# A fourth Strassen unit in the last gate pair, x1's third and fourth quarters ahead of the splits, and the third output group in other banks

## The chip, the cores and the metric

The kernel runs on one core of one Trainium2 chip. The metric is device time in microseconds (us) per execution, the median of the runs; the kernel before takes 807.91 us (three runs, 807.77 to 809.03). Besides the runs there is one profiled execution, whose trace all rows come from. The engines are named as in the profile: PE multiplies matrices (PEld loads its weights), DVE, ACT and POOL work on vectors, SP issues DMA transfers.

## The reference

One layer of a hybrid decoder for 256 tokens of width 2048, all float32. Cut to what matters here:

```python
h = rmsnorm(x, norm_mix_g)
c_g, b_g, xa, za, q, fl, iv, og, ga, gb = split(h @ w_in)
ya = b_g * causal_dwconv3(c_g * xa, conv_w) * silu(za)
log_f = logaddexp(log(lb), log1p(-lb) + log_sigmoid(fl))
kk = (1 - lb) * sigmoid(-fl)
yb = rmsnorm_per_head(hgrn2_chunked(silu(q), kk, iv, log_f)) * silu(og)
m = sigmoid(ga) * (ya @ w_a_out) + sigmoid(gb) * (yb @ w_b_out)
x1 = x + m @ w_o
x2 = x1 + sigmoid(rmsnorm(x1, ple_norm_g) @ w_ple_gate) * (p @ w_ple_proj)
out = rmsnorm(x2, final_norm_g)
```

The change touches the last part of it, from `m @ w_o` to the output, and at one place the `fl` branch.

## The kernel before, in words

**Precision and matmuls.** Each float32 operand is held as two numbers of a shorter type, hi and lo = x - hi, and a product is three matmuls: hi by hi, hi by lo, lo by hi. Activations are the stationary side (128 x 128; names `xh`, `xl` for x1, `mh`, `ml` for m), weights the moving side, 512 columns at a time (`whi`, `wlo`). The 256 tokens are two tiles t = 0, 1, and the 2048 columns of a projection are groups of 512, numbered j.

**Weights.** They stream from memory as `raw` tiles of 1 MB, two chunks of K = 256 each, in three buffers; a new transfer waits until DVE has read the buffer three back. `split` turns a chunk into `whi` on ACT (line 166) and `wlo` on DVE (line 167). Lines 119 to 131 issue the transfers on SP.

**Stages** at the end, in the order of PE's work: OO (output groups 0 and 1 together), O2, O3 (groups 2 and 3 alone), PG0 (gate group 0), GP (gate groups 1 and 2 together), PG3. In the plain groups a chunk is 12 matmuls (line 1258). A stage that takes two groups together follows a written-out program (here `LATE`, line 47) of units (line 1280): `(u, c)` is two chunks for group u, `(2, c)` is one chunk for both, each 24 matmuls; `("S", c)` is one chunk for both groups in Strassen's way: seven products instead of eight, 21 matmuls. For it DVE combines weights in place (`combine_weights`, lines 181, 184, 185), the unit's chunk is split into four parts (three of 1024 columns, one, `t2`, of 512), and the activations enter as *forms* (`So0`, `So1`), which `forms` makes from x1's quarters 0 and 1, one set for each S unit that uses that quarter.

**Sums.** Products of a pair are gathered in banks of two kinds of PSUM tiles, `g` and `s`; `sums` (line 849) adds them up on DVE (the operations appear under `add`, line 845), step by step, as they are finished. For GP `ep_gates_late` then hands each group to `gated` (line 1008): sigmoid on ACT (line 1014), product with `pw` and addition to x (lines 1017, 1018, DVE), squares (line 1019, ACT), and multiplication by the final gain on POOL (line 1026). PG3's first matmuls take over a bank that the first add of GP's sums has read.

**x1's quarters.** When output group j is ready, `ep_o` (line 941) adds it to x (line 845), spreads it (line 947, ACT), takes squares (line 954), and `turned` transposes: four transfers out on SP (line 346, `turn<-t`), one back (line 350, `t<-turn`), and a transposition of 32 x 32 blocks on DVE (line 354). For quarters 2 and 3 `put` then makes `xh` (line 310, ACT) and `xl` (line 311, DVE), four each.

**What sets the order.** Each engine runs its instructions in the order in which they are issued. An epilogue is a generator; the main loop calls `advance` about once per chunk, and every `yield` is a turn's delay; the argument `lag` of `turned` is the number of turns between the way back and the transposition. Splits run ahead of their matmuls by several chunks (`ahead`). For positions in the list of ranges `tied`, `split` is issued after both instructions in `state["splits"]`, the last split before it. Elsewhere a scheduler may place them.

The functions that the change touches, with the line numbers of the profile:

Of the kernel before, what the change touches and what calls it, by code (L numbers as in the profile page):

```python
# [11 lines left out]
AF = mybir.ActivationFunctionType  # L12
# [4 lines left out]
T = 256  # L17
NT = T // P
# [25 lines left out]
INNER = (0, 4), ("S", 0), (0, 6), ("S", 1), (2, 3), ("S", 2), (1, 4), (1, 6)  # L44
FRONT = (0, 2), (0, 4), (0, 6), ("S", 0), (1, 2), ("S", 1), (1, 4), (1, 6)
OUT = (0, 4), ("S", 0), (1, 4), ("S", 1), (2, 3), ("S", 2), (0, 6), (1, 6)
LATE = (0, 4), ("S", 0), (0, 6), ("S", 1), (2, 3), ("S", 2), (1, 4), (1, 6)


PRM_GMIX, PRM_GPLE, PRM_GHG, PRM_LB, PRM_CONV = 0, 16, 32, 40, 48  # L50
# [5 lines left out]
def hybrid_kernel(ctx, tc, xT, x, pT, prm, gfin, masks, w_in, w_a, w_b, w_o, w_pg, w_pp, out):  # L56
    nc = tc.nc
# [23 lines left out]
    state = {"tmp": "tmp1"}  # L81
# [11 lines left out]
    def bank(tag):  # L93
        return ps.tile([P, CW], F32, tag=tag, bufs=4, name=nm(tag))
# [145 lines left out]
    gates, late = of_kind("GG"), of_kind("PG")[0]  # L240
# [6 lines left out]
    tied = []  # L247
# [4 lines left out]
    closing = last_unit("OO", OUT)  # L252
    last = range(gates[-1] + 1, closing + 1)
    outer = range(closing + 6, of_kind("O")[-1] + 1)
    tied.append(range(last[0] - 4, outer[-1] + 1))
    inner = [of_kind(kind) for kind in ("QV", "VG")]
    inner = range(inner[0][0] - 3, inner[0][-1] + 1), range(inner[1][0] - 6, inner[1][-1] + 1)

# [27 lines left out]
    def gain(base, k):  # L286
        return prm_t[:, base + k : base + k + 1]
# [15 lines left out]
    def put(op, k, src, scale=None):  # L303

        hi, lo = op[0][:, k, :], op[1][:, k, :]
        if scale is None:
            nc.scalar.activation(out=hi, in_=src, func=AF.Copy)
            nc.vector.tensor_tensor(out=lo, in0=src, in1=hi.bitcast(F32), op=ALU.subtract)
        else:
            nc.scalar.activation(out=hi, in_=src, func=AF.Identity, scale=scale)  # L310
            nc.vector.scalar_tensor_tensor(  # L311
                out=lo, in0=src, scalar=scale, in1=hi.bitcast(F32), op0=ALU.mult, op1=ALU.subtract
            )


    def rsqrt_of(ss, n, width, tag):
# [20 lines left out]
    def turned(src, lag, dst=None):  # L337

        d = dram.tile([P, 4, T], F32, tag="turn", bufs=3, name=nm("turn"))
        to = d.rearrange("(b i) a x -> a i b x", b=4)
        for a in range(4):
            state["sent"] = nc.sync.dma_start(
                out=to[a], in_=src[32 * a : 32 * a + 32, :].rearrange("i (b x) -> i b x", b=4)
            ).ins
        yield
        nc.sync.dma_start(out=src, in_=d.rearrange("p a x -> p (a x)"))  # L350
        for _ in range(lag):
            yield
        dst = t4() if dst is None else dst
        nc.vector.transpose(  # L354
            out=dst.rearrange("p (k a e) -> p a k e", a=4, e=32), in_=src.rearrange("p (a k e) -> p a k e", a=4, e=32)
        )
        return dst
# [37 lines left out]
    def ep_f(j, psum):  # L395
# [3 lines left out]
        sg = t4()  # L399
# [4 lines left out]
        one, low = (state[n][:, j * 4 : j * 4 + 4] for n in ("oml", "lbm"))  # L404
        for h in range(4):
            s = slice(h * T, (h + 1) * T)
            nc.vector.tensor_scalar(
                out=sg[:, s], in0=sg[:, s], scalar1=one[:, h : h + 1], scalar2=low[:, h : h + 1],
                op0=ALU.mult, op1=ALU.add,
            )  # L410
# [5 lines left out]
            )  # L416
        yield
        yield


        lf, last = t4(), sc(8, "lfl", 2)
        lv, fv = segments(lf), segments(sg)
# [518 lines left out]
    def ep_o(j, psum):  # L941
        xs = state["x"]
        x1 = t4()
        for t in range(NT):
            d = xs[:, t, j * CW : (j + 1) * CW]
            add(d, d, psum[t])
            nc.scalar.activation(out=spread(x1, t), in_=blocks(d), func=AF.Copy)
        turn = turned(x1, 6 if j == 1 else 2)
        next(turn)
        yield  # L950
        junk = t4()
# [18 lines left out]
            yield from forms("x1T", form_tiles(pools["tmp3"], f"So{j}", len(chunks)), r, chunks)  # L970
            return
        for c in range(4):
            put(state["x1T"], j * 4 + c, x1[:, c * T : (c + 1) * T], gain(PRM_GPLE, j * 4 + c))
        if j == 3:
            tot = sc(2, "tot2", 1)
            nc.vector.tensor_reduce(
# [341 lines left out]
    psum = None  # L1318
    for pos, (gi, c) in enumerate(steps[:last_group]):
# [80 lines left out]
                load_projection(1 + c[0] // 2)  # L1400
            continue
        if c == 0:
            psum = [bank("s" if kind == "PP" and j > 1 else "g") for _ in range(NT)]
        hi, lo = parts.pop(pos)
        for i in range(2):
            k = 2 * c + i
# [134 lines left out]
```

## Time and profile before

| | |
|---|---|
| median of three runs | 807.91 us (807.77 to 809.03) |
| the profiled execution | 809.07 us |
| its span, from first to last instruction | 807.3 us |
| mean clock granted to PE | 0.996 |
| busy: PE | 798.0 us, 4169 matmuls |
| busy: DVE | 685.1 us |
| busy: ACT | 492.1 us |
| busy: POOL | 95.4 us |
| HBM over the span | 236 GB/s |

A row of the timeline is: start in us, length in us of the group, engine, line, operation, output <- inputs, shapes, and how many instructions of one kind stand together (xN); in brackets the idle time of the engine ahead of it and what ended that. Matmuls overlap, so their lengths add to more than the time; the distance between starts tells the pace. Rows of transfers give how many, KB each, and us from issue to landing. Rows of stretches give the length, then the busy time and the count of PE, PEld, DVE, ACT and POOL, the granted clock, the share of the DMA engines, and GB/s.

### The profile page before, as it was taken

Reading aid. Unit: us, or ns where it says so; the run is one execution under the profiler, and the core shown is the slowest. Engines: PE = TensorE matmul, PEld = TensorE weight load, DVE = VectorE, ACT = ScalarE, POOL = GpSimd, SP = SyncE. Lnnn points to the kernel's source line nnn. Section 1 sums busy time; section 2 is a strip of 40 time slices with the busy share of each in tenths; the row PEclk is TensorE's granted clock in tenths of the full one; section 3 lists DMA queues with packets and bytes.
Section 4 is the critical chain, followed back from the end, with each engine's and each line's share of the span. In section 5 each row is a group of like instructions: output and inputs, shape, how many; then the busy total and the mean of one; then the engine's idle time right before and its main releaser. Section 6 shows DMA issues by size and latency. Waiting matters only on the chain.

```text
span 807.3 us, 11113 instructions
## 1 busy us (share of the span) xinstructions
PE 798.0 (99%) x4169; PEld 662.3 (82%) x4169; DVE 685.1 (85%) x798; ACT 492.1 (61%) x662; POOL 95.4 (12%) x74
## 2 busy tenths in 40 slices
PE   9999999999999999999999999999999999999995
PEld 7888888888888888888888888888888888887885
DVE  5968897966779987978998998998998988859995
ACT  6967565575656665586674564564565556746562
POOL 0000145300000054300001000000100000002032
PEclk9999999999999999999999999999999999999998
DMA  9899855747676755667584775775875669877542
GB/s 345 295 335 319 268 174 203 237 167 241 240 261 190 261 183 201 209 211 257 189 307 158 227 275 171 239 264 179 275 266 196 208 246 348 327 236 281 205 173 104
DMA packets 50309, 191.20 MB, mean 237 GB/s; under 512 B 5712, under 2 KB 15184, under 8 KB 36304
## 3 DMA queue, kind: packets, MB, share of 16 engines
q1 hardware_dynamic: 50112, 190.24, 68.4%
q8 instruction: 32, 0.52, 0.2%
q10 hardware_dynamic: 144, 0.26, 0.1%
q14 instruction: 21, 0.17, 0.1%
HBM read 175.80 MB, written 14.68 MB: 236 GB/s over the span
## 4 chain that ended last, share of the span: by engine, by line
PE 82%; DVE 10%; issue 2%; DMA 2%; ACT 2%; SPq 0%; POOL 0%; ACTq 0%; POOLq 0%; DVEq 0%
PE g L1258 48%; PE g L1280 25%; PE s L1280 6%; DVE wlo L167 5%; DMA raw<-in_w_pg 2%; ACT whi L166 1%; DVE raw L181 1%; DMA raw<-in_w_o 1%; PE s L1258 1%; PE s L504 1%; DVE t L845 1%; PE s L1131 1%; DVE t L184 1%; DVE t L1017 0%; DVE t L354 0%
## 5 line engine op out<-in xcount | busy, mean ns | idle before, releaser
L167 DVE TENSOR_TENSOR wlo<-raw,whi 128x1024 fp32r<-128x1024 f32 (+1 forms) x320 | 390.2, 1243 | 92.2 <-ACT whi L166 89.4
L166 ACT ACTIVATE whi<-raw 128x1024 fp32r<-128x1024 f32 (+1 forms) x320 | 325.8, 1047 | 175.8 <-PE g L1258 98.3
L1258 PE MATMUL g<-whi,xl 128*128 128x512 f32 (+1 forms) x464 | 177.1, 382 | 0.3 <-DVE xl L311 0.3
L1258 PE MATMUL g<-whi,xh 128*128 128x512 f32 (+1 forms) x464 | 177.4, 383 | 0.0
L1258 PE MATMUL g<-wlo,xh 128*128 128x512 f32 (+1 forms) x464 | 177.1, 382 | 0.0
L1280 PE MATMUL g<-whi,xl 128*128 128x512 f32 x316 | 122.9, 389 | 0.0
L1280 PE MATMUL g<-wlo,xh 128*128 128x512 f32 x316 | 122.9, 389 | 0.0
L1280 PE MATMUL g<-whi,xh 128*128 128x512 f32 x316 | 122.6, 389 | 0.0
L1258 PEld LDWEIGHTS g<-whi,xl 128*128 128x128 f32 x464 | 87.2, 188 | 17.6 <-DVE xl L311 0.8
L1258 PEld LDWEIGHTS g<-whi,xh 128*128 128x128 f32 x464 | 87.2, 188 | 17.0 <-ACT xh L310 0.3
L1258 PEld LDWEIGHTS g<-wlo,xh 128*128 128x128 f32 x464 | 87.3, 188 | 16.8
L166 ACT ACTIVATE whi<-t 128x512 fp32r<-128x512 f32 x25 | 15.8, 632 | 92.1 <-DVE t L184 92.1
L1280 PEld LDWEIGHTS g<-whi,xl 128*128 128x128 f32 x316 | 59.3, 188 | 12.4
L1280 PEld LDWEIGHTS g<-whi,xh 128*128 128x128 f32 x316 | 59.3, 188 | 12.3
L1280 PEld LDWEIGHTS g<-wlo,xh 128*128 128x128 f32 x316 | 59.3, 188 | 12.3
L927 POOL TENSOR_TENSOR t<-ga,gb 128x512 f32<-128x512 f32 x6 | 10.6, 1790 | 188.0 <-issue 118.1
L181 DVE TENSOR_TENSOR raw<-raw 128x1024 f32<-128x1024 f32 x25 | 31.5, 1261 | 0.6
L1258 PE MATMUL g<-whi,yaTh 128*128 128x512 f32 (+1 forms) x74 | 28.2, 388 | 0.0
L1258 PE MATMUL g<-wlo,yaTh 128*128 128x512 f32 (+1 forms) x74 | 27.9, 383 | 0.0
L1258 PE MATMUL g<-whi,yaTl 128*128 128x512 f32 (+1 forms) x74 | 27.9, 383 | 0.0
L1258 PE MATMUL g<-whi,mh 128*128 128x512 f32 x64 | 24.8, 391 | 0.1
L1258 PE MATMUL g<-whi,ml 128*128 128x512 f32 x64 | 24.9, 389 | 0.0
(309 smaller groups left out, 1117.0 us busy)
## 6 DMA issues: line engine op xcount, KB each, us to landing
raw<-in_w_in SPq DMA_DIRECT2D x68, 1024.0 KB, 5.0
raw<-in_w_in SPq DMA_DIRECT2D x37, 512.0 KB, 5.1
raw<-in_w_o SPq DMA_DIRECT2D x12, 1024.0 KB, 6.5
raw<-in_w_pg SPq DMA_DIRECT2D x12, 1024.0 KB, 6.4
raw<-in_w_in SPq DMA_DIRECT2D x38, 256.0 KB, 5.1
turn<-t SPq DMA_DIRECT2D x72, 128.0 KB, 2.8
t<-turn SPq DMA_DIRECT2D x18, 512.0 KB, 5.2
raw<-in_w_a SPq DMA_DIRECT2D x8, 1024.0 KB, 5.6
```

Source lines behind the costliest of these rows:

```text
L166: a = nc.scalar.activation(out=hi[:, s], in_=src[:, s], func=AF.Copy)
L167: v = nc.vector.tensor_tensor(out=lo[:, s], in0=src[:, s], in1=hi[:, s].bitcast(F32), op=ALU.subtract)
L181: nc.vector.tensor_tensor(out=b[:, 0:4:3, :], in0=b[:, 0:3:2, :], in1=b[:, 3:4, :].to_broadcast([P, 2, CW]), op=ALU.subtract)
L184: nc.vector.tensor_tensor(out=t2, in0=b[:, 2, :], in1=b[:, 0, :], op=ALU.add)
L504: nc.tensor.matmul(heads(bk)[r, h, c if at is None else slice(at, at + 32)], key(h)[:, r], query(h)[:, c], start=True, stop=True, tile_pos ...
L845: nc.vector.tensor_tensor(out=out, in0=x, in1=y, op=ALU.add)
L927: (nc.vector if j == 3 else nc.gpsimd).tensor_tensor(out=spread(m, t), in0=blocks(ga[:, s]), in1=blocks(gb[:, s]), op=ALU.add)
L1131: nc.tensor.matmul(wb[:m, :n], *ones, start=True, stop=True)
L1258: nc.tensor.matmul(psum, a, b, start=first and n == 0, stop=last and n == 2)
L1280: nc.tensor.matmul(banks[name], x, y[:, s], start=k == total[name] and i == 0, stop=k == 1 and i == 2)
```

## The change

Six edits. (1) `LATE` has ("S", 2) and ("S", 3) where it had (2, 3) and ("S", 2); a plain unit moves. The S units are four instead of three, So1's forms hold two sets. (2) The second range in `tied`, which ended with the O groups, goes ten positions into PG0. (3) `put` returns its two instructions, and for quarters 2 and 3 they become `state["splits"]`, so that tied splits come after them. (4) The lag of the transposition is 2, 6, 6, 4 turns for quarters 0 to 3, before 2, 6, 2, 2. (5) In `ep_f` for j = 1 the four operations of line 407 go from DVE to ACT, and a turn is added. (6) O2 gathers in `s` banks instead of `g`.

```diff
-LATE = (0, 4), ("S", 0), (0, 6), ("S", 1), (2, 3), ("S", 2), (1, 4), (1, 6)
+LATE = (0, 4), ("S", 0), (0, 6), ("S", 1), (1, 4), ("S", 2), ("S", 3), (1, 6)
...
-    tied.append(range(last[0] - 4, outer[-1] + 1))
+    tied.append(range(last[0] - 4, late + 10))
...
-            nc.scalar.activation(out=hi, in_=src, func=AF.Identity, scale=scale)
-            nc.vector.scalar_tensor_tensor(
+            a = nc.scalar.activation(out=hi, in_=src, func=AF.Identity, scale=scale)
+            v = nc.vector.scalar_tensor_tensor(
                 out=lo, in0=src, scalar=scale, in1=hi.bitcast(F32), op0=ALU.mult, op1=ALU.subtract
             )
+            return a.ins, v.ins
...
         for h in range(4):
             s = slice(h * T, (h + 1) * T)
+            if j:
+                nc.scalar.activation(
+                    out=sg[:, s], in_=sg[:, s], func=AF.Identity, scale=one[:, h : h + 1], bias=low[:, h : h + 1]
+                )
+                continue
             nc.vector.tensor_scalar(
...
         yield
         yield
-
+        if j:
+            yield
...
-        turn = turned(x1, 6 if j == 1 else 2)
+        turn = turned(x1, (2, 6, 6, 4)[j])
...
-            put(state["x1T"], j * 4 + c, x1[:, c * T : (c + 1) * T], gain(PRM_GPLE, j * 4 + c))
+            state["splits"] = put(state["x1T"], j * 4 + c, x1[:, c * T : (c + 1) * T], gain(PRM_GPLE, j * 4 + c))
...
-            psum = [bank("s" if kind == "PP" and j > 1 else "g") for _ in range(NT)]
+            psum = [bank("s" if kind == "PP" and j > 1 or kind == "O" and j == 2 else "g") for _ in range(NT)]
```

The order of instructions moves at three places of which the prediction speaks. Line numbers after the change are up to 7 higher (346 is 347, 354 is 355, 845 is 852).

**SP, around quarter 3's way out.** raw_6271 is PG0's last weights, raw_6326 those of GP's first unit, raw_6376 (6360 in the change) S0's; turn_6278 is quarter 3. Before:

```order
L131 DMA raw_6271<-in_w_pg 128x2048
L346 DMA turn_6278<-t_1114_6273 32x4x256 x4
L131 DMA raw_6326<-in_w_pg 128x2048
L350 DMA t_1114_6273<-turn_6278 128x1024
L119 DMA raw_6376<-in_w_pg 128x1024
L121 DMA raw_6376<-in_w_pg 128x512 x2
L1209 DMA pw_6396<-kept_224 128x1024
```

and after the change:

```order
L131 DMA raw_6271<-in_w_pg 128x2048
L1216 DMA pw_6396<-kept_224 128x1024
L131 DMA raw_6326<-in_w_pg 128x2048
L347 DMA turn_6278<-t_1114_6273 32x4x256 x4
L119 DMA raw_6360<-in_w_pg 128x1024
L121 DMA raw_6360<-in_w_pg 128x512
L351 DMA t_1114_6273<-turn_6278 128x1024
L121 DMA raw_6360<-in_w_pg 128x512
```

The 1 MB of raw_6326 is now issued ahead of quarter 3's four parts, and three quarters of S0's raw ahead of the way back.

**DVE, where quarter 3 is transposed.** Before:

```order
L976 TENSOR_REDUCE tot_1127_6354<-ss_1036_5822 128x2
L167 TENSOR_TENSOR wlo_6361<-raw_6271,whi_6360 128x1024
L319 TENSOR_SCALAR r2v_6356<-tot_1127_6354 128x2
L167 TENSOR_TENSOR wlo_6381<-raw_6271,whi_6380 128x1024
L167 TENSOR_TENSOR wlo_6399<-raw_6326,whi_6398 128x1024
L354 STREAM_TRANSPOSE t_1126_6344<-t_1114_6273 128x4x8x32
L167 TENSOR_TENSOR wlo_6417<-raw_6326,whi_6416 128x1024
L167 TENSOR_TENSOR wlo_6433<-raw_6376,whi_6432 128x1024
L311 TENSOR_SCALAR xl_5826<-t_1126_6344,prm_t,xh_5825 128x256 x4
L181 TENSOR_TENSOR raw_6376<-raw_6376 128x2x512
```

and after the change:

```order
L167 TENSOR_TENSOR wlo_6345<-raw_6271,whi_6344 128x1024
L167 TENSOR_TENSOR wlo_6365<-raw_6271,whi_6364 128x1024
L983 TENSOR_REDUCE tot_1132_6390<-ss_1036_5822 128x2
L320 TENSOR_SCALAR r2v_6392<-tot_1132_6390 128x2
L355 STREAM_TRANSPOSE t_1131_6380<-t_1114_6273 128x4x8x32
L311 TENSOR_SCALAR xl_5826<-t_1131_6380,prm_t,xh_5825 128x256 x4
L167 TENSOR_TENSOR wlo_6399<-raw_6326,whi_6398 128x1024
L167 TENSOR_TENSOR wlo_6417<-raw_6326,whi_6416 128x1024
```

The transposition and the four xl stand ahead of the three splits of raw_6326 and of S0's first part; before, they stood among them.

**DVE, from the last S unit to PG3.** Before, the units after S2's splits were plain (raw_6585, raw_6621), then PG3's first chunks (raw_6656), then the first adds of GP's sums:

```order
L167 TENSOR_TENSOR wlo_6643<-raw_6585,whi_6642 128x1024
L167 TENSOR_TENSOR wlo_6647<-raw_6585,whi_6646 128x1024
L167 TENSOR_TENSOR wlo_6659<-raw_6621,whi_6658 128x1024
L167 TENSOR_TENSOR wlo_6677<-raw_6621,whi_6676 128x1024
L167 TENSOR_TENSOR wlo_6694<-raw_6656,whi_6693 128x1024
L167 TENSOR_TENSOR wlo_6706<-raw_6656,whi_6705 128x1024
L845 TENSOR_TENSOR t_1208_6712<-t_1209_6713,g_6474 128x512
L845 TENSOR_TENSOR t_1209_6713<-t_1209_6713,s_6532 128x512
```

After the change raw_6584 is S3's, raw_6622 the last plain unit's, raw_6661 and raw_6706 PG3's chunks 0 to 3:

```order
L181 TENSOR_TENSOR raw_6584<-raw_6584 128x2x512
L184 TENSOR_TENSOR t_1194_6647<-raw_6584 128x512
L185 TENSOR_TENSOR raw_6584<-raw_6584,t_1194_6647 128x512
L167 TENSOR_TENSOR wlo_6681<-raw_6584,whi_6680 128x1024
L167 TENSOR_TENSOR wlo_6652<-t_1194_6647,whi_6651 128x512
L167 TENSOR_TENSOR wlo_6664<-raw_6584,whi_6663 128x1024
L167 TENSOR_TENSOR wlo_6697<-raw_6622,whi_6696 128x1024
L167 TENSOR_TENSOR wlo_6709<-raw_6622,whi_6708 128x1024
...
L167 TENSOR_TENSOR wlo_6738<-raw_6706,whi_6737 128x1024
L167 TENSOR_TENSOR wlo_6750<-raw_6706,whi_6749 128x1024
L852 TENSOR_TENSOR t_1218_6756<-t_1219_6757,g_6474 128x512
```

S3 brings its combination and a third long split, and the add that reads the bank g_6474 stands behind the splits of PG3's chunks 2 and 3 instead of those of chunks 0 and 1. The other moves: the gate's four operations of PG0 come ahead of S0's last split on DVE instead of behind it, the two adds of O3 stand together, and quarter 2's transposition and xl come one split earlier. In the stage of the `fl` branch the scan of line 434 comes behind a combination (lines 181 to 185) instead of ahead of it.

## The prediction

> **What bounds the kernel now.** I began with the head of the profile's page and its busy times.
>
> ```profile
> span 807.3 us, 11113 instructions
> PE 798.0 (99%) x4169; PEld 662.3 (82%) x4169; DVE 685.1 (85%) x798; ACT 492.1 (61%) x662; POOL 95.4 (12%) x74
> ```
>
> PE is busy for 798.0 of 807.3 us, so the end moves only if PE has fewer matmuls, stands still less, or starts or finishes elsewhere. DVE at 85% is next. The profiled execution took 809.07 us, 1.77 more than its span; the median of the runs is 807.91. I work out a difference on the trace and add it to the median. One measurement tells 0.2% (1.6 us) from no change, no less: "same" below is 806.3 to 809.5.
>
> The chain of waits gives the price of a matmul, and the PE's rows in order of time show where it stands still.
>
> ```profile
> 699.80 12.71 PE g L1258 x56
> ```
> ```profile
> 268.05 0.39 PE L1280 MATMUL g<-whi,xh 128*128 128x512 f32 x1
> 268.46 0.50 PE L1280 MATMUL g<-whi,form 128*128 128x512 f32 x1
> 268.80 0.39 PE L1280 MATMUL s<-whi,form 128*128 128x512 f32 x1
> ...
> 669.12 0.39 PE L1258 MATMUL g<-whi,ml 128*128 128x512 f32 x1
> 669.58 0.50 PE L1258 MATMUL g<-whi,mh 128*128 128x512 f32 x1
> 669.91 0.39 PE L1258 MATMUL g<-wlo,mh 128*128 128x512 f32 x1
> ...
> 730.46 0.39 PE L1280 MATMUL g<-wlo,xh 128*128 128x512 f32 x1
> 730.78 0.50 PE L1258 MATMUL g<-whi,xh 128*128 128x512 f32 x1
> 731.12 0.39 PE L1258 MATMUL g<-wlo,xh 128*128 128x512 f32 x1
> ...
> 732.04 0.40 PE L1280 MATMUL g<-whi,xh 128*128 128x512 f32 x1
> 732.79 0.73 PE L1258 MATMUL g<-whi,xl 128*128 128x512 f32 x2 [0.35 <-DVE xl L311]
> ```
>
> A matmul is 12.71 / 56 = 0.227 us from start to start. What the starts are apart beyond that is lost: 0.18 + 0.11 = 0.30 at 268 (rounded), 0.23 + 0.10 = 0.34 at 669, 0.09 + 0.11 at 731, and 0.52 at 732. The start after 732.79 is hidden in a row of two; I give it the 0.11 that follows the other stops, so 731 and 732 make 0.84. The last is a wait for xl of x1's quarter 3.
>
> **The fourth Strassen unit** replaces 24 matmuls by 21: 3 x 0.227 = **0.68 us** less on PE. On DVE it adds a combination (lines 181, 184, 185) and turns two splits into three long ones and a short one; So1's forms double in width, early, around O3. The price on DVE shows in the work that stands behind quarter 3:
>
> ```profile
> 727.72 1.23 DVE L167 TENSOR_TENSOR wlo<-raw,whi 128x1024 fp32r<-128x1024 f32 x1 [4.26 <-ACT whi L166]
> 728.86 1.24 DVE L354 STREAM_TRANSPOSE t<-t 128x1024 f32<-128x1024 f32 x1
> ...
> 732.25 1.67 DVE L311 SCALAR_TENSOR_TENSOR xl<-t,prm_t,xh 128x256 fp32r<-128x256 f32 x4
> 733.84 1.22 DVE L181 TENSOR_TENSOR raw<-raw 128x1024 f32<-128x1024 f32 x1
> ...
> 736.43 1.22 DVE L167 TENSOR_TENSOR wlo<-raw,whi 128x1024 fp32r<-128x1024 f32 x1
> ...
> 739.30 1.29 DVE L1017 TENSOR_TENSOR t<-t,pw 128x512 f32<-128x512 f32 x2
> ...
> 741.71 3.49 DVE L167 TENSOR_TENSOR wlo<-raw,whi 128x1024 fp32r<-128x1024 f32 x3
> 745.23 2.20 DVE L181 TENSOR_TENSOR raw<-raw 128x1024 f32<-128x1024 f32 x1
> 747.47 1.67 DVE L184 TENSOR_TENSOR t<-raw 128x512 f32<-128x512 f32 x1
> ...
> 749.78 1.22 DVE L167 TENSOR_TENSOR wlo<-raw,whi 128x1024 fp32r<-128x1024 f32 x1
> ...
> 756.17 1.23 DVE L181 TENSOR_TENSOR raw<-raw 128x1024 f32<-128x1024 f32 x1
> ...
> 760.06 6.90 DVE L167 TENSOR_TENSOR wlo<-raw,whi 128x1024 fp32r<-128x1024 f32 x6 [0.48 <-ACT whi L166]
> ```
>
> Three splits go from 741.71 to 745.2, so queued splits are 1.14 apart (the last takes 1.22); the three from 736.43 to 739.30, one of them short, leave 0.6 for the short one; a combination is 733.84 to 736.43 = 2.6, alone. So the unit adds 2.6 + 1.14 + 0.6 = 4.3 us to DVE ahead of PG3, in a stretch where, from 730 to 762, DVE has no more than that 0.48 us free. That is what can eat the gain.
>
> Beside S1, DVE's 181 takes 2.20 and 184 takes 1.67 instead of 1.22 and 0.69, while POOL multiplies by gfin:
>
> ```profile
> 742.48 6.10 POOL L1026 TENSOR_TENSOR xs<-xs,gfin_t 128x512 f32<-128x512 f32 x2 [18.46 <-ACT t L1019]
> ...
> 788.75 2.72 POOL L1026 TENSOR_TENSOR xs<-xs,gfin_t 128x512 f32<-128x512 f32 x2 [2.59 <-ACT t L1019]
> ```
>
> That is 0.98 + 0.98 = 1.96 us, and POOL's two are held up too (6.10 against 2.72). The three splits before are not slowed: POOL got in only when DVE left a hole. In the change the gate's four operations come a little earlier but the next hole is again S1's combination, so I keep 1.96. The Trainium skill's "SBUF — State Buffer", section "Who interferes with whom", says that a DVE operation with two SBUF inputs and a POOL operation that reads SBUF exclude each other for a whole instruction. The rows agree in kind. By it the price could reach POOL's undisturbed 2.72 us, and the forecast would be 0.8 later.
>
> **The stop at 268** waits for a whi that ACT makes late, because DVE's combinations ahead of it are. Moving four operations of line 407 (0.41 us each, 0.33 apart when queued) off DVE gives it 1.3 us, and the scan of line 434 (2.3 us) goes behind a combination instead of ahead. ACT, at 61%, takes the four. I count the **0.30** as gone; 0 is the other end. **The stop at 669** is a matmul of O2 that waits for a g bank that DVE is still to read; the s banks are read before, so **0.34** goes. What would be late next there is wlo, whose tightest cover around O0 and O1 is about half a microsecond.
>
> **Quarter 3 of x1.** Its path is spread by ACT, out through DMA, back, transposed, split.
>
> ```profile
> 717.11 1.78 SPq L346 DMA_DIRECT2D turn<-t  x4
> ```
> ```profile
> turn<-t SPq DMA_DIRECT2D x4, 128.0 KB, 6.0
> ```
> ```profile
> turn<-t SPq DMA_DIRECT2D x4, 128.0 KB, 3.3
> ```
> ```profile
> t<-turn SPq DMA_DIRECT2D x1, 512.0 KB, 3.9
> ```
> ```profile
> t<-turn SPq DMA_DIRECT2D x1, 512.0 KB, 5.6
> ```
>
> The 6.0 is quarter 2's way out (issued from 695.1 on), with a 1 MB raw just ahead; the 3.3 is quarter 3's own, with the raw behind. The 3.9 and the 5.6 are the ways back of quarters 2 and 3. In the change ACT's spreads come 0.8 us earlier (the two adds stand together), so the four parts go out from 716.3 on, the last at 717.65 (a quarter of the 1.78 is the last one's own), but the 1 MB raw is issued before them, near 714.5. DMA then has room:
>
> ```profile
> 710.00:720.00 10.00, 10.00 (x45) 8.29 (x45) 7.69 (x11) 8.52 (x15) 0.00 (x0) 1.00 0.44 149
> ```
>
> (The last columns are the DMA share and GB/s.) The share is 0.44 in that stretch, so I take 3.5 out, near the 3.3, and 3.9 back, since only part of S0's raw stands ahead of it: 717.65 + 3.5 + 3.9 = **725.05**. The ends are 717.65 + 3.3 + 3.9 = 724.85 and 717.65 + 6.0 + 5.6 = 729.25. The transposition and four xl need 1.24 + 1.67 and a first ACT step between, near 0.5: xl is done at 728.5, before PE comes to it (732.04 less 0.34 and the stretch of GP matmuls that no longer stands ahead, about 728.9). So **0.84** goes. The gains are 0.68 + 0.30 + 0.34 + 0.84 = **2.16 us**.
>
> **What is late next.** After 728.5 I lay DVE's rows end to end: 0.5 for a whi that now stands behind ACT's xh (729.0); three splits, 732.4; S0's combination and two splits 2.6 + 1.74 (736.8); the gate's four, 739.30 to 741.71 = 2.4 (739.2); S0's last split (740.35); three splits, 3.5 (743.85); S1's combination under POOL, 745.23 to 749.78 = 4.55 (748.4); 749.78 to 756.17 = 6.4 (754.8); S2, 756.17 to 760.06 and two splits, 3.9 + 2.27 (760.95); S3: a split, 2.6, then 1.14 + 0.6 + 1.22, so 767.7. PE wants S3's last split at 766.9: S2 began at 761.0, is now 0.34 + 0.84 earlier, takes 21 x 0.227 = 4.76, and the split is first used ten matmuls (2.27) into S3. A **new stop of 0.85**, counting a little for the release. S3's raw buffer is free only then, and PG3's chunks 2 and 3 come through it, while in the new order the add that frees PG3's first bank stands behind their splits:
>
> ```profile
> 762.45 4.82 DMA raw<-in_w_pg
> ```
> ```profile
> 770.74 0.68 DVE L845 TENSOR_TENSOR t<-t,g 128x512 f32<-128x512 f32 x1
> ```
> ```profile
> 761.01 0.39 PE L1280 MATMUL s<-whi,xh 128*128 128x512 f32 x1
> ...
> 776.65 0.39 PE L1258 MATMUL g<-whi,xh 128*128 128x512 f32 x1
> ```
>
> Before, that add ended 5.2 us ahead of PG3's start at 776.65. Now: 767.7 + 4.82, a whi 1.06, two splits 2.4, the add 0.68 gives 776.65. PE would be there at 776.65 - 0.68 - 0.34 - 0.84 + 0.85 = 775.65, and waits **1.0** more. PG3 starts when it did. The tail: the last wait of h0's chain (line 1063, ended at 798.8) has 0.96 us before the last add's start at 799.75; the gate's additions come later now and use most of it, so I charge nothing, up to 1 us if they come later still.
>
> ```profile
> 798.63 0.16 DVE L1063 TENSOR_TENSOR xs<-tot,tot 128x1 f32<-128x1 f32 x1 [0.73 <-POOL tot L1062]
> 799.75 0.43 DVE L1035 TENSOR_TENSOR t<-t,pw 128x256 f32<-128x256 f32 x1 [0.96 <-ACT t L1034]
> ```
>
> Sum: -2.16 + 0.85 + 1.0 = -0.3, so 807.91 - 0.3 = **807.6 us** (near 808.8 if the profiled execution is as slow as the one shown). The gains are real, but DVE's chain from quarter 3 to PG3's first bank sets PE's time, and each microsecond of it gives one.
>
> **Rivals.** *The chain is shorter and nothing new is late.* If POOL's multiplies fall into a hole that delays nothing (1.96 less), the add ends at 774.7, and PE, with no stop at S3, is there at 774.8: all 2.16 stand, 805.75. For it: DVE idles 4.26 us before 727.72 in the trace, so holes may appear; against: POOL's start hangs on the gate. From 1.35 us off the chain on it reads as faster. 0.30.
>
> *Quarter 3 comes back late.* If the parts out wait behind the 1 MB raw as quarter 2's did, they need 6.0, and with 3.9 back land at 727.55, 2.5 us later than in my sum. Everything after moves by 2.5, PE stops for quarter 3 longer than before (there are no GP matmuls to fill in), and the time is 810.1. It is slower from a landing near 726.95 on. For it: quarter 2's row; against: DMA's 0.44. The Trainium skill's "DMA: Bandwidth & Descriptors", section "Queues, rings and completion order", says that each DMA engine takes descriptors in ring order, and SP's all share one ring per engine; by it the order of issue decides, which speaks against this change. 0.20, with a late tail in it.
>
> *Only part of it happens:* the stop at 268 stays or the tail takes its 1 us: 807.9 to 808.6, within "same".
>
> **How the numbers follow.** My forecast and the partial case, 0.50, all within 0.2%; faster 0.30; slower 0.20. The range from 805.75, taken as 805.8, leaves out only more than the whole gain; above, it takes in landings to about 727.1, 809.7, and leaves out the worst.
>
> **What would show it.** No stops on PE at 268, 669 and 731; three matmuls fewer. t<-turn landed near 725 and xl done by 728.9. Line 181 near 2.2 at S1. A stop of PE inside S3 for wlo, and one at PG3's first matmul for the add of line 845. Wrong: if DVE is ahead at S3 and PG3 starts near 774.8 (faster), or if xl stops PE again (slower).

## The result and the profile after

The changed kernel takes **811.45 us** (median of six runs, 810.68 to 812.27), the kernel before 808.4 us in six runs beside them (807.77 to 810.36): ratio **1.0038**, 95% interval 1.0027 to 1.0048. It is 3.05 us slower; 807.6 was forecast, with no difference from the kernel before that could be told. The profiled execution of the change took 810.68 us, which is also the lowest of its runs, with a span of 808.9 and a granted clock of 0.997. On the traces the difference is therefore only 808.9 - 807.3 = 1.6 us, and the other half of it has to be looked for in what differs between executions.

The head of the page, and the busy times:

```profile
span 808.9 us, 11118 instructions
PE 797.1 (99%) x4165; PEld 661.3 (82%) x4166; DVE 690.9 (85%) x799; ACT 496.0 (61%) x668; POOL 92.4 (11%) x74
```

PE is busy for 0.9 us less, the span is longer by 1.6: PE stands still for longer, or what follows it takes longer. The view by stretches shows where. Its rows are start and end; length; busy time and count of PE, PEld, DVE, ACT, POOL; granted clock; share of the DMA engines; GB/s. From S0 to PG3 it was, before:

```profile
740.00:777.00 37.00, 37.00 (x165) 30.65 (x164) 34.67 (x35) 22.59 (x28) 6.10 (x2) 1.00 0.67 242
```

and is after:

```profile
740.00:777.00 37.00, 35.57 (x152) 27.62 (x150) 34.72 (x33) 21.18 (x27) 7.05 (x2) 1.00 0.64 233
```

There PE was busy for all of 37.00 us before, now for 35.57. Where the old stops were, it is busy without a gap now (10.00 us in each of the stretches 260 to 270, 660 to 670 and 730 to 740; before 9.97, 9.93 and 9.65), and its matmuls start 0.22 to 0.23 apart: the old stops are gone. PE's waits name what it waits for (total, times, longest), and its rows in order of time show the places:

```profile
PE s L1287 <- DVE wlo L167: 1.0, 3, 0.7
PE g L1265 <- DVE t L852: 0.7, 1, 0.7
```
```profile
750.46 0.39 PE L1287 MATMUL s<-whi,So0h 128*128 128x512 f32 x1
750.84 0.50 PE L1287 MATMUL s<-wlo,So0h 128*128 128x512 f32 x1
...
751.41 0.40 PE L1287 MATMUL s<-whi,So0h 128*128 128x512 f32 x1
751.98 0.50 PE L1287 MATMUL s<-wlo,So0h 128*128 128x512 f32 x1 [0.17 <-DVE wlo L167]
...
766.16 0.39 PE L1287 MATMUL s<-whi,So1h 128*128 128x512 f32 x1
767.25 0.50 PE L1287 MATMUL s<-wlo,So1h 128*128 128x512 f32 x1 [0.69 <-DVE wlo L167]
...
767.82 0.39 PE L1287 MATMUL s<-whi,So1h 128*128 128x512 f32 x1
768.38 0.50 PE L1287 MATMUL s<-wlo,So1h 128*128 128x512 f32 x1 [0.17 <-DVE wlo L167]
...
776.22 0.39 PE L1287 MATMUL g<-whi,xl 128*128 128x512 f32 x1
777.34 0.50 PE L1265 MATMUL g<-whi,xh 128*128 128x512 f32 x1 [0.73 <-DVE t L852]
777.67 0.39 PE L1265 MATMUL g<-wlo,xh 128*128 128x512 f32 x1
```

Against a pace of 0.227, PE loses 0.15 and 0.34 us inside S1, 0.86 and 0.33 inside S3 and 0.89 at PG3's first matmul, and about 0.11 at the matmul after each stop: 0.7, 1.4 and 1.0. Every releaser is DVE. DVE, in turn, hangs on quarter 3 of x1, whose way shows in SP's rows and in the rows of transfers:

```profile
714.51 0.33 SPq L131 DMA_DIRECT2D raw<-in_w_pg  x1
715.52 1.82 SPq L347 DMA_DIRECT2D turn<-t  x4
...
722.09 0.33 SPq L351 DMA_DIRECT2D t<-turn  x1
```
```profile
turn<-t SPq DMA_DIRECT2D x4, 128.0 KB, 5.3
t<-turn SPq DMA_DIRECT2D x1, 512.0 KB, 3.4
```

The four parts, issued after the 1 MB raw, took 5.3 us (median; the last, issued at 715.52 + 3/4 of 1.82 = 716.9, landed at 722.1, 5.2 later), and the way back 3.4: landed at 725.5. Then DVE:

```profile
725.51 1.25 DVE L355 STREAM_TRANSPOSE t<-t 128x1024 f32<-128x1024 f32 x1 [5.18 <-DMA t<-turn]
...
727.34 1.69 DVE L311 SCALAR_TENSOR_TENSOR xl<-t,prm_t,xh 128x256 fp32r<-128x256 f32 x4 [0.58 <-ACT xh L310]
...
729.48 3.50 DVE L167 TENSOR_TENSOR wlo<-raw,whi 128x1024 fp32r<-128x1024 f32 x3 [0.46 <-ACT whi L166]
733.01 1.23 DVE L181 TENSOR_TENSOR raw<-raw 128x1024 f32<-128x1024 f32 x1
...
744.41 2.20 DVE L181 TENSOR_TENSOR raw<-raw 128x1024 f32<-128x1024 f32 x1
746.64 1.68 DVE L184 TENSOR_TENSOR t<-raw 128x512 f32<-128x512 f32 x1
...
776.60 0.68 DVE L852 TENSOR_TENSOR t<-t,g 128x512 f32<-128x512 f32 x1
...
790.85 1.28 DVE L1025 TENSOR_TENSOR xs<-xs,t 128x512 f32<-128x512 f32 x2
...
801.36 0.16 DVE L1070 TENSOR_TENSOR xs<-tot,tot 128x1 f32<-128x1 f32 x1 [0.73 <-POOL tot L1069]
801.44 0.42 DVE L1042 TENSOR_TENSOR t<-t,pw 128x256 f32<-128x256 f32 x1
```

Three things are to be seen. DVE now stands idle for 5.18 us until quarter 3 has landed, with the splits that it could make queued behind it. From the transposition's start to S0's combination (line 181) it is 733.01 - 725.51 = **7.50 us**, with two holes in which it waits for ACT, where the old order needed 733.84 - 728.86 = 4.98. And the delay outlasts PG3's start: GP's last additions start at 790.85. Before, they started 3.6 us earlier:

```profile
787.24 1.28 DVE L1018 TENSOR_TENSOR xs<-xs,t 128x512 f32<-128x512 f32 x2
```

At the very end it is DVE that is waited for. ACT's last sigmoid,

```profile
800.06 0.47 ACT L1041 ACTIVATE t<-g,r2r 128x256 f32<-128x256 f32 x1 [0.75 <-PE g L1265]
```

is ready at 800.53, but its product on DVE starts at 801.44, behind h0's chain; before, that chain had ended and DVE waited 0.96 for the sigmoid. From PG3's start to the end it is 808.9 - 777.34 = 31.56 us, before 807.3 - 776.65 = 30.65.

### The profile page after: what moved, and what is told of

It reads as the page before. It is cut to its first block, busy times and chain, and to the rows that moved or that the text cites. A ratio compares the mean times of both kernels' runs of the same rounds, so it can differ in the third digit from the quotient of the medians.

```text
span 808.9 us, 11118 instructions
## 1 busy us (share of the span) xinstructions
PE 797.1 (99%) x4165; PEld 661.3 (82%) x4166; DVE 690.9 (85%) x799; ACT 496.0 (61%) x668; POOL 92.4 (11%) x74
## 5 line engine op out<-in xcount | busy, mean ns | idle before, releaser
L1287 PE MATMUL g<-wlo,xh 128*128 128x512 f32 x310 | 120.6, 389 | 0.0
L1287 PE MATMUL g<-whi,xl 128*128 128x512 f32 x310 | 120.6, 389 | 0.0
L1287 PE MATMUL g<-whi,xh 128*128 128x512 f32 x310 | 120.1, 389 | 0.0
L1265 PE MATMUL g<-whi,ybTh 128*128 128x512 f32 x64 | 24.9, 389 | 0.0
L1265 PE MATMUL g<-wlo,ybTh 128*128 128x512 f32 x64 | 24.9, 389 | 0.0
```

Of the source, the lines that this page charges most:

```text
L1265: nc.tensor.matmul(psum, a, b, start=first and n == 0, stop=last and n == 2)
L1287: nc.tensor.matmul(banks[name], x, y[:, s], start=k == total[name] and i == 0, stop=k == 1 and i == 2)
```

## The experiments

The theory after this reading: DVE's chain from quarter 3's landing to the end sets the time; the fourth unit makes the chain longer, and the new order hangs its start on a transfer. Rivals: the stop at PG3's first matmul, a matter of banks, is what costs; the fourth unit costs by itself, wherever quarter 3 stands; POOL's multiplies are the price. The kernel before was timed anew beside each kernel, and its median moves (808.16 to 809.34), so small differences are read from the ratios.

**1. The fourth unit undone** (e1: the change with the old program).

```diff
-LATE = (0, 4), ("S", 0), (0, 6), ("S", 1), (1, 4), ("S", 2), ("S", 3), (1, 6)
+LATE = (0, 4), ("S", 0), (0, 6), ("S", 1), (2, 3), ("S", 2), (1, 4), (1, 6)
```

> The changed kernel with three Strassen units again (LATE as before), all other edits kept. Theory A (the chain on DVE from quarter 3's way back to PG3's first bank and on to the tail is over-full, and the fourth unit's 4.3 us on it cost more than its 0.68 us of PE): the stops inside S3 (1.4 us), at PG3's first matmul (1.0) and the later tail (0.9) go, 0.68 comes back on PE, so 808.8 us or a little less, against 811.45. The small stops at S0 and S1 (0.8 together) stay. Theory B (the new order around quarter 3 is what costs; the fourth unit pays its 0.68): 812.1 us.

Measured: 808.47 us beside 808.16, ratio 1.0002 (0.9994 to 1.0011). As theory A had it, all of the loss goes with the fourth unit. But the other five edits, which take 1.5 us of stops from PE, leave the time where it was. Of PE's waits in the stages that changed, one line is left:

```profile
PE s L1287 <- DVE wlo L167: 0.3, 2, 0.2
```

The line counts idle time alone. By the starts of the matmuls, PE loses 0.44 us at S0 and 0.72 inside S1, 1.16 together, so most of the 1.5 is lost again there.

**2. The fourth unit alone** (e2: the kernel before, with the new program).

```diff
-LATE = (0, 4), ("S", 0), (0, 6), ("S", 1), (2, 3), ("S", 2), (1, 4), (1, 6)
+LATE = (0, 4), ("S", 0), (0, 6), ("S", 1), (1, 4), ("S", 2), ("S", 3), (1, 6)
```

> The kernel before with the fourth Strassen unit alone. Theory A: S3's last split ends near 769.0 and PE wants it at 768.0, a stop of about 1.2 with the pause after it; the add that frees PG3's first bank ends near 778, another 0.8; the tail 0.9 later; less 0.68: 2.2 us slower than before, 810.6 us. Theory B: 0.68 faster, 807.7 us.

Measured: 810.4 us beside 808.16, ratio 1.0024 (1.0013 to 1.0035), about +1.95 us. PE's waits, in the old order too, are those of the change; only the last one is the old stop of quarter 3:

```profile
PE g L1258 <- DVE t L845: 0.8, 1, 0.8
PE s L1280 <- DVE wlo L167: 0.7, 2, 0.5
PE g L1258 <- DVE xl L311: 0.4, 1, 0.4
```

So the unit costs about 2 us in the old order, too, as theory A had it: it brings more DVE work than PE saves. With the other edits around it, it is 1.0038 for the change against 1.0002 without the unit. That looks like more, but 0.0036 and 0.0024 can't be told apart within their intervals.

**3. The parts out ahead of the weights** (e3: GP's weights, too, are issued after the last part out).

```diff
-        if unit_of[pos] not in loaded and groups[steps[pos][0]][0] == "O":
+        if unit_of[pos] not in loaded and groups[steps[pos][0]][0] in ("O", "GP"):
```

> The changed kernel with one edit: the 1 MB of GP's first weights is issued after quarter 3's four parts out instead of ahead of them; the order on DVE is the same. Theory A: the parts land 1.5 to 2 us earlier (out in 3.3 us instead of 5.2 after the last issue), the whole chain starts that much earlier, the stops at S0 and S1 go, and S3's and PG3's shrink: 1.2 to 1.8 us faster, 809.7 to 810.2 us. Theory B, or a start of the chain that doesn't matter: 811.4 us, no change.

Measured: 811.12 us beside 808.16, ratio 1.0034 (1.0021 to 1.0048): no gain, where theory A expected 1.2 to 1.8 us, a **miss**. The transfers say why:

```profile
turn<-t SPq DMA_DIRECT2D x4, 128.0 KB, 2.6
t<-turn SPq DMA_DIRECT2D x1, 512.0 KB, 5.6
```

The parts out now need 2.6 instead of 5.3, but the raw stands right ahead of the way back, which takes 5.6 instead of 3.4. The transposition starts at 726.94, no earlier. The wait behind the weights only moved from one leg to the other.

**4. POOL's gain multiplies left out for gate group 0** (e4; they are the two that stood beside S1's combination).

```diff
-        for t in range(NT):
+        for t in range(NT if j else 0):
```

> The changed kernel without POOL's two multiplications by the final gain for gate group 0 (that part of the output lacks the gain). Theory A: lines 181 and 184 of S1 take 1.23 and 0.69 again, 1.96 us less on the chain after S1; the stops at S1 and S3 go or shrink and PG3's first matmul comes 1.5 to 2 us earlier: 809.5 us. Theory B, or a chain with room to spare: 811.4 us.

Measured: 810.33 us beside 808.16, ratio 1.0026 (1.0015 to 1.0037): less gained than theory A expected. At S1 DVE's operations are back to their undisturbed time, but an addition of the next group is now hit:

```profile
746.82 1.23 DVE L181 TENSOR_TENSOR raw<-raw 128x1024 f32<-128x1024 f32 x1
...
787.62 1.78 DVE L1025 TENSOR_TENSOR xs<-xs,t 128x512 f32<-128x512 f32 x1
```

That is 1.23 (and 0.69 for line 184) against 2.20 and 1.68 beside POOL, and 1.78 against 0.68 for line 1025, where POOL's next pair starts at 786.85. The 1.10 us lost there is more than half of the 1.96 gained at S1. The Trainium skill's "SBUF — State Buffer", section "Who interferes with whom", says that a DVE operation with two SBUF inputs and a POOL operation that reads SBUF contend, and that the order of issue decides which one is blocked; these rows agree in kind.

**5. PG3's first half bank from the other kind** (e5), so that its first matmul doesn't wait for the add.

```diff
-        bk, n = bank("g"), CW // 2
+        bk, n = bank("s" if t == 0 else "g"), CW // 2
```

> The changed kernel with one edit: PG3's first pass gathers in an s bank, which ACT copies out before the add on DVE that frees the g bank. Theory A as it stood in the prediction (PE's stop at PG3 is on the path that sets the end): that stop of 1.0 us shrinks to a few tenths and the time falls by as much, to 810.6 us. Theory A2 (behind S3 the end is set by DVE itself: sums, gates and h0's chain, which finish 0.9 us after h1's sigmoid is ready): PE's stop shrinks, but the time stays at 811.4.

Measured: 812.07 us beside 808.54, ratio 1.0043 (1.0031 to 1.0055). At PG3's start PE goes on without a stop:

```profile
777.48 0.39 PE L1287 MATMUL g<-whi,xl 128*128 128x512 f32 x1
777.71 0.39 PE L1265 MATMUL s<-whi,xh 128*128 128x512 f32 x1
```

The stop of 1.0 us is gone, and the time isn't better. PE stops later instead, inside PG3 at 788.05 and for a split of DVE:

```profile
PE s L1265 <- DVE wlo L167: 0.4, 1, 0.4
```

This rules out the bank as the cause: PE only waited where DVE was late anyway.

**6. Splits less far ahead in GP** (e6), so that the adds stand earlier on DVE.

```diff
-        return LEAD + min(max(pos - late - 4, 0) // 3, 5) + n
+        return LEAD + min(max(pos - late - 4, 0) // 3, 3) + n
```

> The changed kernel with splits that run at most three chunks further ahead at the end of GP instead of five: the first add of GP's sums comes before the splits of PG3's chunks 2 and 3. Theory A and A2 alike: the add ends near 773.5, PE's stop at PG3 goes (1.0) and the gates and the tail come some 2 us earlier (0.9): 809.5 us. If instead a split of PG3 becomes late, no gain: 811.4 or more.

Measured: 811.67 us beside 808.54, ratio 1.0037 (1.0025 to 1.0048). The 809.5 of both theories didn't come; it is the other branch. The add moves up to 775.11, and instead PE waits inside PG3 for a split:

```profile
785.56 0.39 PE L1265 MATMUL g<-whi,xh 128*128 128x512 f32 x1
786.81 0.50 PE L1265 MATMUL g<-wlo,xh 128*128 128x512 f32 x1 [0.86 <-DVE wlo L167]
```

GP's last additions do come earlier, 791.35 - 727.84 = 63.5 us after the transposition's start instead of 790.85 - 725.51 = 65.3, but PE loses 1.7 us inside PG3 (1.13 here, 0.59 at 788.4). From the transposition to the end of the span it is 811.2 - 727.84 = 83.4 us, as in the change. The order on DVE decides where PE stops. That the amount of DVE's work decides how late the end is would fit, but this run alone doesn't show it.

**7. The last unit's combination cut down** (e7: lines 181 and 185 are left out for it).

```diff
+        bare = groups[steps[pos][0]][0] == "GP" and steps[pos][1][0] == 6
+        if not bare:
...
+        if not bare:
```

> The changed kernel without lines 181 and 185 for the fourth Strassen unit (its weights enter uncombined; 21 matmuls as before): 1.9 us less DVE work at S3 and nothing else taken away; one split of S3 moves earlier. Theory A: the stop inside S3 (1.4) and PG3's (1.0) go or nearly so, and the tail moves by up to 0.9: 808.5 to 809.5 us. If the fourth unit costs by something other than DVE's time: 811.4 us.

Measured: 811.44 us beside 808.54, ratio 1.0034 (1.0022 to 1.0046). This is a **miss** of the theory: 1.9 us of DVE's work were taken away, and 808.5 to 809.5 was expected. The rows show that DVE was given other work ahead of the unit's last split:

```profile
765.02 1.22 DVE L167 TENSOR_TENSOR wlo<-raw,whi 128x1024 fp32r<-128x1024 f32 x1
...
766.75 2.35 DVE L167 TENSOR_TENSOR wlo<-raw,whi 128x1024 fp32r<-128x1024 f32 x2
...
774.22 2.36 DVE L167 TENSOR_TENSOR wlo<-raw,whi 128x1024 fp32r<-128x1024 f32 x2 [2.48 <-ACT whi L166]
...
799.48 0.42 DVE L1045 TENSOR_TENSOR t<-t,pw 128x256 f32<-128x256 f32 x1 [0.45 <-ACT t L1044]
```

The split at 765.02 belongs to the plain unit behind; in the change it came after S3's. S3's last split is the first of the two at 766.75, and its buffer's next transfer is issued at 768.00, 41.78 us after the transposition's start (726.22). In the change that is 768.35 - 725.51 = 42.84, so 1.06 of the 1.9 us came through. The transfer then takes as long as it did (5.0, in the change 4.8), and DVE stands idle for 2.48 us, waiting for the whi made from it, where it did for 1.46 in the change; the wait for the add at PG3 stays (1.0 in the waits). GP's last additions start at 790.74, 64.52 us after the transposition instead of 65.34, so 0.82 us is still there. It is lost in the tail, which stands in another order: the third of the last products with pw comes behind the scaling of the first token tile, at 799.48, where the change has it ahead, at 797.11, in a wait for POOL. From the last additions to the end it is 809.7 - 790.74 = 19.0 us, in the change 808.9 - 790.85 = 18.05, and from the transposition to the end 83.5, no less than in the change. So between S3 and PG3 the chain isn't DVE's work alone: it runs through the buffer and its transfer. And since the order changed with the work, the run can't say how much of the 1.9 us would have reached the end in the change's order.

**8. Both legs of quarter 3 ahead of the weights** (e8: as e3, and for quarter 3 what GP's weights are issued after is the way back).

```diff
-        if unit_of[pos] not in loaded and groups[steps[pos][0]][0] == "O":
+        if unit_of[pos] not in loaded and groups[steps[pos][0]][0] in ("O", "GP"):
...
-    def turned(src, lag, dst=None):
+    def turned(src, lag, dst=None, late_turn=False):
...
-        nc.sync.dma_start(out=src, in_=d.rearrange("p a x -> p (a x)"))
+        back = nc.sync.dma_start(out=src, in_=d.rearrange("p a x -> p (a x)"))
+        if late_turn:
+            state["sent"] = back.ins
...
-        turn = turned(x1, (2, 6, 6, 4)[j])
+        turn = turned(x1, (2, 6, 6, 4)[j], None, j == 3)
```

> The changed kernel with quarter 3's way out and way back both issued ahead of the weights of GP's first unit and of S0; the order on DVE is the same. If the way back was late because it shares the queues with the weights around it: out 4 us, back 3.9 us, landed at 725 in every run instead of 725.5 to 727.9, xl 0.5 to 2 us earlier, and with theory A the time falls by 1 to 1.5 us, to 810.2. If the landing does not set the start of the chain, or the weights then come too late: 811.4 or more.

Measured: 809.65 us beside 808.54, ratio 1.0010 (1.0002 to 1.0019) against the change's 1.0038 (1.0027 to 1.0048): about 1.8 us below the change's median (2.3 by the ratios), with the four units.

```profile
turn<-t SPq DMA_DIRECT2D x4, 128.0 KB, 2.5
t<-turn SPq DMA_DIRECT2D x1, 512.0 KB, 3.6
```
```profile
723.98 1.25 DVE L357 STREAM_TRANSPOSE t<-t 128x1024 f32<-128x1024 f32 x1 [3.65 <-DMA t<-turn]
```

With nothing ahead of them the legs take 2.5 and 3.6, the transposition starts at 723.98, and the end comes earlier by as much: from the transposition to the end of the span it is 807.2 - 723.98 = 83.2 us, in the change 808.9 - 725.51 = 83.4. This is the run that shows the first half of the theory. The Trainium skill's "DMA: Bandwidth & Descriptors", section "Queues, rings and completion order", says that on each DMA engine descriptors are consumed in ring order. What the two runs measure agrees: the way back takes 5.6 right behind the raw (e3) and 3.6 ahead of it (e8).

**9. Both legs ahead, with three units** (e9: the edits of e1 and e8 together).

```diff
-LATE = (0, 4), ("S", 0), (0, 6), ("S", 1), (1, 4), ("S", 2), ("S", 3), (1, 6)
+LATE = (0, 4), ("S", 0), (0, 6), ("S", 1), (2, 3), ("S", 2), (1, 4), (1, 6)
...
+        if late_turn:
+            state["sent"] = back.ins
```

> The changed kernel with three Strassen units and with quarter 3's way back ahead of the weights (e1 and e8 together). If DVE's chain from the way back on is what PE waits for at S0 and S1 in e1 (1.2 us of stops there), an earlier landing takes these and all five other edits show their gain: 807.0 to 807.4 us, 1.1 to 1.5 under e1 and about 1 under the kernel before. If e1's lost gain is elsewhere: 808.4.

Measured: **807.37 us** beside 808.59, ratio 0.9988 (0.998 to 0.9997): faster than both kernels, if by little. Behind its warm-up PE has no wait for another engine, and from S0 to PG3 it is busy throughout:

```profile
740.00:777.00 37.00, 37.00 (x165) 30.65 (x164) 34.51 (x34) 22.56 (x25) 6.39 (x2) 1.00 0.61 228
```

Here the other edits' gain, 807.3 - 805.7 = 1.6 us of span (about 1.0 by the ratio), at last arrives.

The change, e1, e8 and e9 make a square. Both legs first are worth 0.0014 of the time with three units (1.0002 to 0.9988) and 0.0028 with four (1.0038 to 1.0010). The fourth unit costs 0.0036 with quarter 3 late and 0.0022, about 1.8 us, with it early. So both causes count by themselves: an early quarter 3 doesn't make the unit pay.

**10. Both legs ahead, in the kernel before** (e10).

```diff
-        turn = turned(x1, 6 if j == 1 else 2)
+        turn = turned(x1, 6 if j == 1 else 2, None, j == 3)
```

(and the other lines of e8's edit.)

> The kernel before with quarter 3's way back ahead of the weights of GP's first unit, and nothing else (the transposition then stands ahead of three splits on DVE by itself). The stops at 731 and 732 (0.84 us) go, DVE's chain starts 2 to 3 us earlier than before and has more room: 807.4 us, 0.8 under the kernel before. If the landing is no bound there: 808.2.

Measured: 809.87 us beside 808.59, ratio 1.0015 (1.0006 to 1.0023): slower, where 807.4 was expected, a **miss**. The transposition starts at 726.93, on landing, since the way back now followed two transfers of pw (512 KB each, issued at 718.35) and took 5.4. And with the weights issued later, the splits that used to stand ahead of it stand behind:

```profile
726.93 1.25 DVE L356 STREAM_TRANSPOSE t<-t 128x1024 f32<-128x1024 f32 x1 [4.07 <-DMA t<-turn]
...
734.52 1.23 DVE L181 TENSOR_TENSOR raw<-raw 128x1024 f32<-128x1024 f32 x1
```

From the transposition to the combination it is 7.59 us, the length of the new order, not the old order's 4.98. Without meaning to, the run repeats the change's loss in the kernel before: quarter 3 first and landing late costs.

**11. All of POOL's gain multiplies left out** (e11: three groups, six operations).

```diff
-        for t in range(NT):
+        for t in range(0):
```

> The changed kernel without POOL's six multiplications by the final gain (three of four column groups of the output lack the gain). In the six profiles of kernels with four units the end came 82.7 to 83.7 us after quarter 3's landing, with or without PE's stop at PG3's first matmul. If this is DVE's chain, 1.96 us at S1 and 0.8 at the gates before the tail leave it: end 80.6 to 81.4 us after the landing, 808.5 to 809.5 us. If the chain has room: 811.4.

Measured: 809.35 us beside 808.59, ratio 1.0007 (0.9994 to 1.0019), inside the 808.5 to 809.5 expected. The second place is free now, too:

```profile
788.50 1.31 DVE L1024 TENSOR_TENSOR t<-t,pw 128x512 f32<-128x512 f32 x2 [0.21 <-ACT t L1021]
```

1.31 for two, in the change 2.17. In this trace quarter 3 came as late as 727.24, and the span is still 807.8: from the transposition to the end 80.6 us, not 83.4. Of the 2.8 us, 2.0 are gained up to PG3's first matmul (777.09 - 727.24 = 49.85 instead of 51.83) and 0.8 behind it (30.72 instead of 31.56). Work taken off DVE moves the end, and part of it stands behind PG3's start.

**12. Three units, and the splits not tied** (e12).

```diff
-LATE = (0, 4), ("S", 0), (0, 6), ("S", 1), (1, 4), ("S", 2), ("S", 3), (1, 6)
+LATE = (0, 4), ("S", 0), (0, 6), ("S", 1), (2, 3), ("S", 2), (1, 4), (1, 6)
...
-    tied.append(range(last[0] - 4, late + 10))
+    tied.append(range(last[0] - 4, outer[-1] + 1))
```

> The changed kernel with three Strassen units (LATE as before) and the second tied range as before, so that quarter 3's transposition and xl stand among the splits again and its parts go out ahead of the weights; left of the change are line 407 on ACT, O2's banks and the lags. If the new place of quarter 3 only moves the loss (PE's 0.84 at 731 is gone, but DVE's chain begins with holes and PE stops at S0 and S1 instead), this kernel keeps the 0.64 of the stops at 268 and 669 and is at 807.6 us, as good as or better than e1 (808.5), with the stop at 731 back and none at S0 and S1. If the new place is a gain in itself: 809 us or more.

Measured: 808.12 us beside 809.34, ratio 0.9992 (0.9982 to 1.0003). The stop at 731 was expected back; it wasn't there:

```profile
726.65 1.24 DVE L355 STREAM_TRANSPOSE t<-t 128x1024 f32<-128x1024 f32 x1
...
731.63 1.22 DVE L181 TENSOR_TENSOR raw<-raw 128x1024 f32<-128x1024 f32 x1
```

Without the tie, the splits fill ACT's holes, the combination starts 4.98 us after the transposition, and PE has no stop. The span is 805.7, that of e9, though quarter 3 is transposed 2.5 us later than there. But the median can't be told from the kernel before, nor from e1.

## Why the prediction was wrong, point by point

**The stops that go, the matmuls that go: right.** The stops at 268, 669, 731 and 732 are gone, three matmuls went with the unit. What failed is how much of these 2.16 us was left as a gain: the prediction itself said that DVE's chain sets PE's time, and then the gain counts only as far as DVE is not late. It charged 1.85 us of new stops. On the traces there are 3.2 (0.1 at S0, 0.7, 1.4 and 1.0) and 0.9 more in the tail. In e9, which has no fourth unit and where DVE is in time, 1.6 us of span arrive.

**The chain from quarter 3 to PG3: right in kind, and nearly in size.** From the landing to PG3's first matmul it was laid end to end as 776.65 - 725.05 = 51.60 us, and measured as 777.34 - 725.49 = 51.85. S1's combination under POOL took the 2.20 and 1.68 assumed. The stop inside S3 is there, 1.4 instead of 0.85, and the one at PG3, 1.0 as forecast. That the second agrees is luck: on the change's own clock PE came to PG3 at 776.45 (forecast 775.35) and the add ended at 777.28 (forecast 776.35), both about 1 us later. S1's 0.7 was not foreseen: the prediction asked whether DVE was ahead only at S3.

**The way out: the step that failed first.** "So I take 3.5 out, near the 3.3", it said, because the DMA engines were busy for only 0.44 of the ten us around. A share over 10 us says nothing of what stands directly ahead. The row of quarter 2, 6.0 behind a raw, was the right one to go by: measured were 5.2 for the last part, against 2.5 and 2.6 with nothing ahead (e8, e3). On the change's own clock, 0.30 earlier for the stop at 268, the landing was forecast at 725.05 - 0.30 = 724.75 and came at 725.49: 0.45 earlier by the issue, 1.7 later by the way out, 0.5 earlier by the way back, together 0.74. Most of the 0.45 is no merit of the change: its profile is 0.35 ahead already at the matmul before the old stop at 268 (267.70 against 268.05).

**The tail: charged nothing, measured 0.91.** The prediction saw the gate's additions come later, and that the last chain had 0.96 us to spare, and let the spare take it. But with four units DVE enters PG3 with a backlog (the last additions at 790.85 instead of 787.24), and the spare was gone and more: 31.56 - 30.65 = 0.91 us.

These add up on the trace: 0.74 + 0.25 + 0.91 = 1.9 us, from the 807.0 that was forecast for the span (807.3 - 0.3) to the 808.9 measured.

**The other half lies between a profile and the median.** The prediction added the trace's difference to the median, as if both profiled executions were alike. The kernel before was profiled at 809.07, 0.67 above the 808.4 of its six runs; the change at 810.68, 0.77 below its median. And 808.4 itself is 0.5 above the 807.91 of three runs that the forecast started from: 1.9 + 0.67 + 0.77 + 0.5 make the 3.85 us between 807.6 and 811.45.

What spreads in the change is in part the landing. In the seven profiles of kernels with the raw ahead of the parts (the change, e1, e4, e5, e6, e7, e11) the transposition starts between 725.51 and 727.93, each time on landing, and the change's is the earliest. In the order before, 728.86 was not bound by it. How much hangs on the landing shows in the time from the transposition to the end of the span: 83.4 in the change, 83.7, 83.3, 83.4, 83.5 and 83.2 in e3, e5, e6, e7 and e8, whether the landing was at 724.0 or at 727.8, and whether PE stopped at PG3 or not (82.7 and 80.6 in e4 and e11, where DVE loses less beside POOL). So with four units each microsecond of landing is one of the end. By this, and 810.68 - 808.9 = 1.78 around the span, the median 811.45 would be a landing near 726.3; that is an estimate, since only profiled executions show the landing. That all of the 0.77 is the landing isn't shown, and the 0.67 seems to have another source: the runs of the kernel before spread as far (807.15 to 810.74 in the 23 beside e1), though its profile isn't bound by the landing.

**The rivals.** "Quarter 3 comes back late" had the mechanism: the parts wait behind the raw. Its numbers were not those of the profile, though. It put the landing at 727.55, and 725.49 was measured; it had PE stop for quarter 3, and in the change's profile PE doesn't. In those with a landing from 726.8 on PE does (0.54 us in e5, 1.49 in e4 at 727.93). Its 810.1 was short for want of the tail, and its point of decision, a landing at 726.95, was too kind. Simply from the rows: with 7.50 us from the landing to S0's combination, the new order is ahead of the old one's 733.84 only if quarter 3 lands by 726.3, and then there is still the unit to pay. "The chain is shorter" was wrong: POOL's multiplies met S1's combination much as before (7.05 us for the two, 6.10 before).

**What stays open.** In the seven profiles the way out goes with the head start of the raw, the time from the raw's issue to the first part's:

| | e4 | e6 | e5 | change | e11 | e7 | e1 |
|---|---|---|---|---|---|---|---|
| head start of the raw, us | 0.45 | 0.64 | 0.90 | 1.01 | 1.17 | 1.67 | 1.68 |
| way out, us (median of four) | 6.6 | 5.7 | 5.4 | 5.3 | 5.3 | 4.2 | 4.0 |

The closer the raw stands, the longer the way out. The two add up to 5.7 to 7.1 us, and the raw itself lands 4.9 to 5.8 us after its issue in these profiles, as if the parts landed soon after it. Why the raw is issued sooner in one execution than in another, and why the way back takes 3.4 to 4.8, isn't shown. e7 met a new order before PG3 and another one in the tail, so the unit's 4.3 us on DVE were never taken out alone, and which of them count is not known. No run takes POOL's multiplies out of the kernel before, so e11 shows what they cost the change, not that this cost came with the change. And the 1.95 us of the unit by itself and the rest's 0.3 (808.47 - 808.16) don't make 3.05; the missing 0.8 is about what the spread of the landing could do, but it is also within the intervals, and no run separates it.

## What to carry to other kernels

When two engines are each nearly full, price a change on both, and count a stop removed on the one as a gain only as far as the other is ahead there: three matmuls fewer (0.68 us of PE) were bought with 4.3 us of DVE. Before work is put in order behind a transfer, look at what that transfer queues behind, leg by leg, not at the mean load; and move both legs of a round trip, or the wait only changes legs. A landing that sets the time also brings its own spread, and a profiled execution need not be the median of its kernel: place each profile among its runs before a difference of two traces is added to a median.

## What the runs showed of the hardware

A transfer of 128 KB took 2.5 to 2.6 us from issue to landing with nothing right ahead in e3, e8 and e9 (3.2 to 3.5 before and in e2, e10 and e12) and 4.0 to 6.6 (medians of four) behind a raw of 1 MB that the same engine issued 0.45 to 1.7 us earlier, longer the closer the raw stood. One of 512 KB took 3.5 to 3.6 with nothing right ahead (e8, e9), 3.4 to 4.8 in the seven profiles with part of a raw ahead, and 5.4 to 5.7 right behind 1 MB (before, e2, e3, e10; 4.3 in e12). The spread of the landing from one profile to the next, 2.4 us, was nearly as large as the effect under study (3.05); 0.84 of it is there before the first part is issued (715.42 to 716.26). And DVE's slowing beside POOL moved, when POOL's operations were taken away in one place, to the next pair (e4), and went only when all were gone (e11).
